# A second token mixer reorganised into a phase of paired block products and a phase of values, gates and small products

## The chip, the cores and the metric

The kernel runs on one core of one Trainium2 chip. The metric is the time on the device in microseconds (us), the median of several runs. The engines are named as in the profile: PE is the matrix engine (PEld its weight loads), DVE the vector engine, ACT the scalar engine, POOL the general engine, SP the engine that issues the DMAs. PE writes to PSUM, eight banks of 128 x 512 float32 elements. All other on-chip data lies in SBUF, 128 partitions wide.

## What is computed

A decoder trunk of two layers on 1024 tokens of width 1024. Layer 0 has a gated DeltaNet and a short convolution, layer 1, which this change concerns, has HGRN2 and dilated attention. Each layer ends with a SwiGLU feed-forward part of 2816 hidden columns. Cut to what matters:

```python
def mixer_cd(h, w_in, lower_bound, norm_g, w_out):          # h: 1024 x 1024, already normed
    hq, hf, hi, hg, sq, sk, sv = split_cols(h @ w_in, CD_SPLITS)   # 4 x 512 and 3 x 1536 columns
    f_gate = lb + (1.0 - lb) * sigmoid(hf)
    k_in = (1.0 - lb) * sigmoid(-hf)
    o_c = hgrn2_recurrence(silu(hq), k_in, hi, log(f_gate))  # 4 heads of 128, a chunked recurrence
    o_c = rms_norm(o_c, norm_g) * sigmoid(hg)
    sq, sk = rope(sq), rope(sk)                              # 3 patterns x 4 heads of 128
    for p, (window, dilation) in enumerate(((128, 1), (512, 4), (2048, 16))):
        outs[p], lses[p] = dilated_window_attention(sq[p], sk[p], sv[p], window, dilation)
    o_d = sum over p of outs[p] * softmax(lses)[p]
    return concatenate([o_c, o_d]) @ w_out
```

## The kernel before

**Products in three terms.** Activations and weights are float32. Each is split into a high part (a cast on ACT, line 101) and a low part (a subtraction on DVE, line 102), and a product is three matmuls: high by high, high by low, low by high (lines 125 to 127). A column block is 128 output columns with all 1024 rows of depth, that is 8 depth steps. The 1024 tokens are two halves of 512. So a column block costs 2 x 8 x 3 = 48 matmuls of 512 columns.

**The feed-forward part** (class `Up`, from line 251) already does less. It takes two column blocks at once, a gate and an up block, as a 2 x 2 block product (column block by depth half) with the 2 x 2 blocks of the activations (depth half by token half), with seven block products in place of eight and sums and differences around them: weights get the sums s1 to s4 (POOL, lines 296 to 302), activations the sums t1 to t4 (`turn`, line 586 on DVE). The names a11, a12, a22 are weight blocks, b11, b21, b22 activation blocks. `pair` is one round: p1, p2, row 2, row 1, p6, p5, p7, where PE's, DVE's, ACT's, POOL's and, after the first rounds, SP's instructions stay in the order in which they are written (`manual_schedule`).

**The second mixer** (`mixer_cd`, from line 1375) does not. In it the order is set by a planner, which lays the instructions of each engine in a row beforehand, by their priority (the order in which the program names them) and by planned durations. On the chip each engine then goes through its row and waits where an input is late. The program names the work as wide products with small work between them:

- `hgrn_fq`: forget and query tiles of an HGRN2 head, two column blocks.
- `hgrn_v`: HGRN2 values of two heads, 128 tokens at a time, matmuls of 256 columns.
- `swa_v`: attention values of a pattern for four heads, matmuls of 512 columns.
- `swa_qk`: query and key blocks of one head and pattern, then the rotary step (lines 1656 to 1663: two copies on ACT that swap the halves, two products and a sum on DVE), kept in SBUF.
- `hgrn_gates`: the gates of HGRN2.

Between wide products `tick(cost)` lets two generators go one step each per unit of cost: `chain`, the HGRN2 units (a head and a token half) in ten steps (`hgrn`, lines 1452 to 1600: forget preparation with a reciprocal at 1458 and a scan at 1461, seven levels of decayed copies at 1473 to 1481, small products at 1489 to 1595), and `local`, the attention (`Attend`: scores at 1706 with the masked minimum at 1713, transposes at 1752, outputs at 1763, and for pattern 0 the merge of the three patterns at 1801 to 1824). A unit of cost is one token half of a column block, 24 matmuls. The output projection (`out_proj`) needs all tiles of a token half from DRAM, attention tiles first.

PSUM banks have three tags: g (2 banks, HGRN2 steps), u (3 banks, wide products) and m (3 banks, attention).

## Time and profile before

| what | value |
|---|---|
| three runs | 2606.16, 2606.19 and 2607.6 us; median 2606.19 us |
| profiled execution, first to last instruction (its span) | 2604.6 us, so 1.6 us less than the median run |
| PE busy | 2585.2 us, 99%, 14355 matmuls |
| DVE, ACT, POOL busy | 1651.8, 1006.9 and 462.6 us |
| data moved by DMA | 402.98 MB |
| second mixer, 1155 to 1862 us | 707.00 us, with DVE busy 446.96 us |

The page of the profile has busy totals, then the span in 40 slices with a digit for the busy tenths of each engine, then the chain of work that ended last. The view by windows gives busy time and counts of each engine in stretches of time; the view by line gives groups of instructions with their total and mean duration and the idle time before them. A matmul's recorded duration is longer than its distance from the next one, since they are pipelined.

### The profile page before, as it was taken

What the parts mean: (1) busy time and instruction counts of PE and PEld (TensorE: products, weight loads), DVE (VectorE), ACT (ScalarE), POOL (GpSimd) and SP (SyncE); (2) the same over time, 40 slices, a digit from 0 to 9 for tenths busy, and PEclk for the clock granted to TensorE, in tenths of its full rate; (3) what the DMA queues carried; (4) which work ended last, traced back from release to release, by engine and by line L of the source; (5) the groups of instructions that cost most, each with busy time, mean ns of one, the idle gap of its engine ahead of it and who ended that gap; (6) DMA issues with size and microseconds to landing.
All of it is one profiled execution on the core that took longest, in us unless ns stands there. A gap on an engine that the chain in (4) does not pass through costs nothing.

```text
span 2604.6 us, 37378 instructions
## 1 busy us (share of the span) xinstructions
PE 2585.2 (99%) x14355; PEld 2159.7 (83%) x14355; DVE 1651.8 (63%) x2816; ACT 1006.9 (39%) x1679; POOL 462.6 (18%) x436
## 2 busy tenths in 40 slices
PE   8999999999999999999999999999999999999998
PEld 6888888888888888888888888888888888888887
DVE  7887776585656665564665557578567565566554
ACT  5432123343333345333444335444444333334442
POOL 1110121334333300010000000000024433331001
PEclk9999999999999999999999999999999999999999
DMA  4434446424556688541212222224652555568853
GB/s 143 134 103 151 123 143 202 166 88 163 183 186 202 217 292 293 189 134 62 81 62 74 86 70 62 86 70 126 219 195 68 174 174 200 204 205 284 281 173 120
DMA packets 239827, 402.98 MB, mean 155 GB/s; under 512 B 30208, under 2 KB 114720, under 8 KB 239520
## 3 DMA queue, kind: packets, MB, share of 16 engines
q1 hardware_dynamic: 239648, 400.59, 46.3%
q8 instruction: 113, 1.85, 0.3%
q14 instruction: 66, 0.54, 0.1%
HBM read 280.36 MB, written 120.14 MB: 154 GB/s over the span
## 4 chain that ended last, share of the span: by engine, by line
PE 95%; DVE 3%; issue 1%; ACT 0%; DMA 0%; POOL 0%; SPq 0%; POOLq 0%; DVEq 0%; ACTq 0%
PE psu L125 20%; PE psu L127 20%; PE psu L126 20%; PE psg L125 5%; PE psg L127 5%; PE psg L126 5%; PE psm L127 4%; PE psm L125 4%; PE psm L126 4%; PE psm L1763 1%; PE psm L1706 1%; PE psg L1489 1%; PE psm L198 1%; DVE h L586 1%; PE psm L1752 0%
## 5 line engine op out<-in xcount | busy, mean ns | idle before, releaser
L125 PE MATMUL psu<-hnh,w 128*128 128x512 f32 x1328 | 531.0, 400 | 7.1 <-ACT w L101 7.1
L127 PE MATMUL psu<-hnh,w 128*128 128x512 f32 x1328 | 520.1, 392 | 0.0
L126 PE MATMUL psu<-hnl,w 128*128 128x512 f32 x1328 | 519.2, 391 | 0.5 <-DVE hnl L1928 0.5
L102 DVE TENSOR_TENSOR w<-raw,w 128x1024 fp32r<-128x1024 f32 (+1 forms) x314 | 372.3, 1187 | 154.6 <-ACT w L101 152.5
L101 ACT CAST w<-raw 128x1024 fp32r<-128x1024 f32 (+1 forms) x314 | 306.1, 976 | 301.5 <-PE psu L127 153.4
L125 PEld LDWEIGHTS psu<-hnh,w 128*128 128x128 f32 x1328 | 250.4, 189 | 57.1 <-ACT w L101 7.1
L127 PEld LDWEIGHTS psu<-hnh,w 128*128 128x128 f32 x1328 | 249.9, 188 | 53.9 <-DVE w L102 0.8
L126 PEld LDWEIGHTS psu<-hnl,w 128*128 128x128 f32 x1328 | 250.5, 189 | 50.2 <-DVE hnl L1928 1.1
L186 POOL TENSOR_TENSOR acc<-acc,sq 128x512 f32<-128x512 f32 x48 | 70.6, 1471 | 497.9 <-ACT sq L182 497.9
L102 DVE TENSOR_TENSOR hidq<-hr,hidq 128x1024 fp32r<-128x1024 f32 x72 | 82.4, 1146 | 71.2 <-ACT hidq L101 70.8
L296 POOL TENSOR_TENSOR ws<-raw 128x512 f32<-128x512 f32 x40 | 54.4, 1360 | 356.3 <-DMA raw<-in_dram 254.2
L125 PE MATMUL psu<-w,hnh 128*128 128x512 f32 (+1 forms) x320 | 113.3, 354 | 0.0
L102 DVE TENSOR_TENSOR w<-ws,w 128x1024 fp32r<-128x1024 f32 x38 | 49.7, 1308 | 98.9 <-ACT w L101 98.9
L127 PE MATMUL psu<-w,hnl 128*128 128x512 f32 (+1 forms) x320 | 111.4, 348 | 0.0
L126 PE MATMUL psu<-w,hnh 128*128 128x512 f32 (+1 forms) x320 | 111.3, 348 | 0.0
L101 ACT CAST hidq<-hr 128x1024 fp32r<-128x1024 f32 x72 | 70.2, 980 | 97.3 <-DMA hr<-ts 56.8
L125 PE MATMUL psm<-hidq,w 128*128 128x512 f32 (+1 forms) x275 | 106.1, 386 | 0.0
L127 PE MATMUL psm<-hidq,w 128*128 128x512 f32 (+1 forms) x275 | 106.0, 385 | 0.0
L126 PE MATMUL psm<-hidq,w 128*128 128x512 f32 (+1 forms) x275 | 106.0, 385 | 0.0
L1527 POOL COPY attn<-ac 32x128 f32<-32x128 f32 x32 | 12.8, 401 | 433.3 <-DVE ac L1493 380.5
L125 PE MATMUL psu<-hidq,w 128*128 128x512 f32 (+1 forms) x220 | 84.7, 385 | 0.0
L127 PE MATMUL psu<-hidq,w 128*128 128x512 f32 (+1 forms) x220 | 84.6, 384 | 0.0
(451 smaller groups left out, 5744.9 us busy)
## 6 DMA issues: line engine op xcount, KB each, us to landing
raw<-in_dram SPq DMA_DIRECT2D x228, 512.0 KB, 3.7
sd<-in_dram SPq DMA_DIRECT2D x44, 512.0 KB, 3.8
hid<-hid SPq DMA_DIRECT2D x88, 256.0 KB, 2.9
sd<-sd SPq DMA_DIRECT2D x44, 512.0 KB, 3.3
hr<-ts SPq DMA_DIRECT2D x40, 512.0 KB, 4.6
raw<-sd SPq DMA_DIRECT2D x40, 512.0 KB, 3.9
hd<-h SPq DMA_DIRECT2D x48, 256.0 KB, 4.0
h<-hd SPq DMA_DIRECT2D x48, 256.0 KB, 5.8
```

The lines of the kernel that those rows point to most:

```text
L101: S.copy(hi, src)
L102: eng.tensor_tensor(lo, src, hi.bitcast(F32), op=SUB)
L125: T.matmul(o, lh, rh, start=first and i == 0, stop=False, **kw)
L126: T.matmul(o, lh, rl, start=False, stop=False, **kw)
L127: T.matmul(o, ll, rh, start=False, stop=last and i == n - 1, **kw)
L186: (eng or G).tensor_tensor(a, a, q, op=ADD)
L198: T.matmul(st[:, j:j + 1], x[:, j * P:(j + 1) * P], onesn, start=i + j == 0, stop=i == 1, skip_group_check=True)
L296: G.tensor_tensor(s[:, HT:], b[:, :HT], b[:, HT:], op=ADD)
L586: eng.tensor_tensor(dst, x, y, op=SUB)
L1489: T.matmul(od[r * 32:(r + 1) * 32, c * 32:(c + 1) * 32], a[:, z], x[:, z], start=True, stop=True, tile_position=(0, r * 32))
L1706: T.matmul(o[:, z], self.q[:, j * P:(j + 1) * P], self.k[:, (j - m + 1) * P:(j + 1) * P], start=True, stop=True)
L1763: T.matmul(po[:, jj * P:(jj + 1) * P], pt[:, z.start + i * P:z.start + (i + 1) * P], self.vp[:, j - m + 1 + i, :], start=i == 0, stop=i == ...
```

## The change

Before the mixer's values, a new class `Pairs` goes through 16 pairs of column blocks with the seven block products of `Up`: 12 pairs are the query and key blocks of a head and pattern, 4 are the forget and query blocks of an HGRN2 head. The four results of a pair (two blocks by two token halves) are finished by generators that are stepped between the products: `roped`, `forget` and `query`. One of the two rotary products moves from DVE to POOL. The finished tiles are stored to DRAM. `turn` now ends in a method `ends`, which each class has for itself, and hands one block of activations (b12) to `upper`, which stores it; at the end of the pairs it is loaded again into the tiles of t1, so that the normed activations are whole for the values.

`mixer_cd` then has values, gates and all small products. `ask` loads the tiles of an HGRN2 unit, `Attend` loads its own queries, keys and values, one head and pattern ahead. The scan, which ran over 512 columns with a mask that reset it, runs in four pieces of 128 in `forget`. `tick` now counts for the two generators at different rates, and its costs are in half units of before (12 matmuls). The gates are made head by head, both token halves.

```diff
+    class Pairs(Up):
+        early = True
+        HEADS = (("k", 0, 0), ("k", 0, 1), ("k", 0, 2), ("k", 0, 3), ("k", 1, 0), ("f", 0), ("k", 1, 1), ("k", 1, 2),
+                 ("f", 1), ("k", 1, 3), ("k", 2, 0), ("f", 2), ("k", 2, 1), ("k", 2, 2), ("f", 3), ("k", 2, 3))
...
+        def upper(self, b12):
+            dma(self.b12, b12)
...
+        def done(self, f, i, half, c, psum=False):
+            kind = self.HEADS[f]
+            if kind[0] == "k":
+                return self.roped(self.qk[kind[1:]][i, :, half], kind[1], half, c, psum)
+            if i == 0:
+                return self.forget(self.bkq[kind[1], half], kind[1], c)
+            return self.query(self.bkq[kind[1], half], c, psum)
+
+        def roped(self, dst, p, half, c, psum):
+            t = slice(half * HT, (half + 1) * HT)
+            r = self.turned()
+            S.copy(r[0:64], c[64:128])
+            S.copy(r[64:128], c[0:64])
+            G.tensor_tensor(r, r, self.rope[:, 1, t], op=MULT)
+            V.tensor_tensor(c, c, self.rope[:, 0, t], op=MULT)
+            yield
+            if p == 0:
+                d = r if psum else c
+                V.tensor_tensor(d, c, r, op=ADD)
+            else:
+                n = (None, 4, 16)[p]
+                d = self.scratch("d")
+                V.tensor_tensor(d.rearrange("p (r i) -> p i r", r=n), c.rearrange("p (i r) -> p i r", r=n),
+                                r.rearrange("p (i r) -> p i r", r=n), op=ADD)
+            dma(dst, d)
+            yield
+
+        def forget(self, dst, h, c):
+            r = self.turned()
+            V.tensor_scalar(c, c, -44.0, None, op0=MAX)
+            S.activation(r, c, AF.Exp, scale=-1.0)
+            S.activation(c, r, AF.Identity, bias=onec[:, 0:1])
+            yield
+            V.reciprocal(c, c)
+            d = self.scratch("d")
+            G.tensor_tensor(d, r, c, op=MULT)
+            yield
+            S.activation(r, c, AF.Ln, scale=self.omlb[:, h:h + 1], bias=self.lb[:, h:h + 1])
+            S.activation(d, d, AF.Copy, scale=self.omlb[:, h:h + 1])
+            dma(dst[1], d)
+            yield
+            for j in range(4):
+                t = slice(j * P, (j + 1) * P)
+                V.tensor_tensor_scan(c[:, t], onec[:, 0:1].to_broadcast([P, P]), r[:, t], 0.0, op0=MULT, op1=ADD)
+            dma(dst[0], c)
+            yield
...
+        def pair(self, f, count, b11, b21, b22, t1, t2, t3, t4):
+            n = f + 1
+            more = n < count
+            self.p1(f, b11)
+            self.add22(f - 1)
...
+                an = self.next
+                bn = self.raw("u", n, n % 3 == 2)
+            c = self.done(f - 1, 1, 1, self.c22.pop(f - 1))
+            next(c)
+            self.p2(f, b21, psm())
+            g = self.snap(f)
+            next(self.tail, None)
+            next(c)
+            next(self.tail, None)
...
+            if more:
+                s = self.sums(an, bn)
+            self.add11(f, g)
+            g = self.done(f, 0, 0, self.g1.pop(f))
+            next(g)
+            if more:
+                self.part_a(n, an)
+            x = self.row2(f - 1, t4)
+            next(x)
+            next(g)
+            z = self.row1(f - 1, b22)
+            next(x)
+            if more:
+                self.sums_late(an, bn, s)
+                if f > 3:
+                    self.part_b(n, s)
+            self.p6(f, t2)
...
+            next(z)
+            next(g, None)
+            self.p5(f, t1, psg())
+            if more:
+                if n + 1 < count:
+                    self.next = self.raw("g", n + 1, (n + 1) % 3 == 1)
+                slow = self.HEADS[f - 1][0] == "f"
+                if slow:
+                    next(z)
+                self.part_c(n, bn)
+                self.part_d(n, an)
+                next(g, None)
...
+                self.tail = z
+                self.p7(f, t3)
+                return
...
-    def mixer_cd(hn, hp, second, close):
+    def mixer_cd(hn, hp, pairs):
...
-                    tick(0.5)
+                    tick(1)
...
+            def ask(u):
+                if u < 8:
+                    h, half = divmod(u, 2)
+                    raws[u] = [hl(n, bufs=2) for n in ("b", "kk", "q")]
+                    for i, t in enumerate(raws[u]):
+                        dma(t, pairs.bkq[h, half][i])
...
-            def hgrn_gates():
+            def hgrn_gates(tick):
                 ws = [wload(("cd", 12 + 2 * i), ("cd", 13 + 2 * i)) for i in range(2)]
-                for half in range(NH):
-                    for h in range(4):
-                        oc = hl("e4", bufs=3)
+                for h in range(4):
+                    for half in range(NH):
+                        o = proj(wk(ws[h // 2], h % 2), hn[half], range(KH), last=False)
+                        tick(1)
+                        proj(wk(ws[h // 2], h % 2), hn[half], range(KH, KT), o, first=False)
+                        xg = hl("xg", bufs=2)
+                        S.activation(xg, o, AF.Tanh, scale=0.5)
+                        tick(1)
+                        while done_c[0] <= 2 * h + half:
+                            next(hg_chain, None)
+                        oc = hl("oc")
                         dma(oc, scr_g[half, h])
...
-                        tick(0.75 if len(tts) > 1 else 1)
+                        tick(1.5 if len(tts) > 1 else 2)
...
-                def __init__(self, h, p, q, k, vp):
+                def __init__(self, h, p):
+                    self.h, self.p = h, p
+                    for i, n in enumerate("qk"):
+                        t = tl(n, (2, HT), 2)
+                        if p == 2 and i == 0:
+                            t4 = t.rearrange("p b t -> p (b t)").rearrange("p (s b i) -> p b s i", s=16, b=2)
+                            for b in range(2):
+                                dma(t4[:, b], pairs.qk[p, h][i, :, b].rearrange("p (s i) -> p s i", s=16))
+                        else:
+                            dma(t, pairs.qk[p, h][i])
+                        setattr(self, n, t)
+                    self.vp = values(h, p)
...
-            acc = [0.0]
+            due, rate = [0.0, 0.0], [0.0, 4 / 3]
 
             def tick(cost):
+                for i in range(2):
+                    due[i] += cost * rate[i]
+                while max(due) >= 1:
+                    for i, work in enumerate((loc, hg_chain)):
+                        if due[i] >= 1:
+                            due[i] -= 1
+                            next(work, None)
...
+            hgrn_v(0, pairs.first, lambda cost: None, range(0, 4))
+            have_v[0] = 1
+            hgrn_v(0, pairs.first, tick, range(4, 8))
             for p in (1, 2, 0):
                 swa_v(p, tick)
-                feed_hgrn()
-                for h in range(4):
-                    q, k = swa_qk(h, p, tick)
-                    ready.append([Attend(h, p, q, k, values(h, p)), 0])
-                    feed_hgrn()
...
+                ready += [(h, p) for h in range(4)]
+                rate[0] = 1.4 if p == 0 else 0.8
+                if p == 2:
+                    hgrn_v(1, wload(("cd", 10), ("cd", 11)), tick)
+                    have_v[0] = 2
+            hgrn_gates(tick)
             while ready or busy[0]:
                 next(loc)
```

More of the change, by code (lines that the diff above doesn't have):

```diff
@@ L252, in hybrid_trunk_kernel @@
     class Up:
+        early = False
         def __init__(self, layer, left):
@@ L1859, in local @@
                     line = [line[1], nxt]
-                    busy[0] = any(line) or bool(late)
+                    busy[0] = any(line) or bool(late or now or ahead or ready)
                     yield
```

340 lines of the change are left out of this document (216 added, 124 removed).

## The prediction

> **What bounds the kernel now.** The page first: engine totals, slices, and the chain that ended last.
>
> ```profile
> span 2604.6 us, 37378 instructions
> PE 2585.2 (99%) x14355; PEld 2159.7 (83%) x14355; DVE 1651.8 (63%) x2816; ACT 1006.9 (39%) x1679; POOL 462.6 (18%) x436
> PE   8999999999999999999999999999999999999998
> DVE  7887776585656665564665557578567565566554
> PEclk9999999999999999999999999999999999999999
> PE 95%; DVE 3%; issue 1%; ACT 0%; DMA 0%; POOL 0%; SPq 0%; POOLq 0%; DVEq 0%; ACTq 0%
> ```
>
> PE is busy in every slice at the full granted clock, and the chain is PE for 95%. A busy PE need not be a PE at its rate, so next come stages, from the view by windows: the turn of the first feed-forward part, the pairs that follow it, the whole second mixer, and a piece near its end.
>
> ```profile
> core 0: us, PE busy (x) PEld busy (x) DVE busy (x) ACT busy (x) POOL busy (x), PEclk, DMA share, GB/s
> 530.00:565.00 35.00, 34.27 (x150) 27.74 (x149) 34.75 (x33) 18.19 (x23) 9.51 (x3) 1.00 0.16 51
> 565.00:980.00 415.00, 415.00 (x1833) 343.88 (x1832) 250.03 (x322) 150.87 (x204) 132.24 (x98) 1.00 0.61 207
> 1155.00:1862.00 707.00, 707.00 (x5378) 598.76 (x5379) 446.96 (x1043) 307.27 (x639) 26.23 (x51) 1.00 0.27 84
> 1740.00:1780.00 40.00, 40.00 (x416) 34.13 (x415) 36.88 (x106) 23.03 (x53) 2.15 (x4) 1.00 0.31 93
> ```
>
> Between 565 and 980 all products have 512 columns: 415.00/1833 = 0.2264 us each. The gate multiplications on POOL come once a pair there; the first and the fourth of a run of four:
>
> ```profile
> 702.06 1.29 POOL L387 TENSOR_TENSOR hid<-hid,c 128x512 f32<-128x512 f32 x1 [0.18 <-ACT hid L386]
> ...
> 759.18 1.29 POOL L387 TENSOR_TENSOR hid<-hid,c 128x512 f32<-128x512 f32 x1 [0.36 <-ACT hid L386]
> ```
>
> Three pairs in 57.12 us are 19.04 each, and 84 x 0.2264 = 19.02: the scheme that the change extends already runs without a stall in this kernel. In the mixer I count 1,536 products of 512 columns for queries, keys, forget tiles and HGRN2 queries, 576 for attention values and 192 for gates: 2,304 x 0.2264 = 521.6 of 707 us; the narrow value products and small ones are the other 185. PE never lacks work there, so removed products come off the end, as long as what remains still has cover.
>
> **The sum.** A pair of column blocks costs 2 blocks x 2 halves x 8 depths x 3 terms = 96 products now, and 7 x 4 x 3 = 84 as block products. 16 pairs save 192 x 0.2264 = **-43.5 us**. Against it:
>
> *Turn.* Building the four sums of activations is the same code as before the feed-forward pairs. Its window above has 150 products, 34.0 us of work in 35.00, with DVE busy 34.75. The second half's norm, which it takes in, was in the old mixer too. I add **+1** (0 to +2).
>
> *Phase one: 16 pairs on in-order queues.* DVE costs are read from a dense piece of its timeline, since recorded spans overlap:
>
> ```profile
> 1229.33 0.43 DVE L1477 TENSOR_TENSOR m<-m,kk 128x256 f32<-128x256 f32 x1
> 1229.67 0.42 DVE L1481 TENSOR_TENSOR m<-m,q 128x256 f32<-128x256 f32 x1
> 1230.01 0.69 DVE L1539 TENSOR_TENSOR kk<-kk,b 128x512 f32<-128x512 f32 x1
> 1230.61 0.69 DVE L1534 TENSOR_TENSOR q<-q,t 128x512 f32<-128x512 f32 x1
> ```
>
> Starts are 0.34 us apart for 256 columns and 0.60 for 512, about 0.09 below the spans. So I take 0.09 off the means of the groups by line (mixer window):
>
> ```profile
> L102 DVE TENSOR_TENSOR w<-raw,w 128x1024 fp32r<-128x1024 f32 x55 | 67.3, 1223 | 46.3 <-ACT w L101 46.2
> L101 ACT CAST w<-raw 128x1024 fp32r<-128x1024 f32 x54 | 56.6, 1047 | 26.4 <-PE psu L127 22.0 <-DMA raw<-in_dram 3.9
> L1659 DVE TENSOR_TENSOR sw<-sw,rope 128x512 f32<-128x512 f32 x48 | 33.1, 690 | 31.1 <-ACT sw L1657 29.0 <-DMA vp<-scr_v 1.8
> L1656 ACT COPY sw<-psu 64x512 f32<-64x512 f32 x48 | 28.0, 583 | 120.7 <-PE psu L127 87.0 <-issue 33.2 <-ACT attn L1524 0.4
> L1458 DVE RECIPROCAL b<-b 128x512 f32<-128x512 f32 x8 | 26.8, 3352 | 0.2
> L1473 DVE TENSOR_TENSOR m<-b 128x256 f32<-128x256 f32 x56 | 23.2, 420 | 24.4 <-PE psg L1489 24.1
> L1663 DVE TENSOR_TENSOR k<-psu,sw 128x512 f32<-128x512 f32 x24 | 22.9, 954 | 0.2
> L1461 DVE TENSOR_TENSOR_SCAN b<-rmask,t 128x512 f32<-128x512 f32 x8 | 9.8, 1222 | 4.8 <-ACT t L1460 4.7
> ```
>
> DVE per query/key pair: 3.5 splits of 1.13 (4.0), three additions of 0.60 (1.8), four rotated tiles of 0.60 + 0.87 (5.9): 11.7 of 19.0 us, 62%, where the feed-forward pairs have 250.03/415 = 60% and no stall. POOL takes one rotary product a tile; with four weight sums that is 8 x 1.29 = 10.3 of 19.0, and the weight sums queued behind them have half a pair to spare. ACT: 3.5 casts of 1.05, and three copies and eight half-height copies of 512 columns at 0.58: 10.1.
> A forget pair has 4.0 + 1.8 + 2 x (0.60 + 3.35 + about 1.5 for the scan in four pieces) + 2 x 0.60 = 17.9 on DVE. Forget pairs are three apart: (17.9 + 2 x 11.7)/57 = 72%. What queues behind the 3.35 us reciprocal is the next pair's weight splits, which PE reads at least four products (10.9 us) later, and the additions that free a PSUM bank. Cover gone, eight reciprocals would cost 27 us; I add **+2** (0 to +13, four exposed).
> SP gets some 72 more stores of 256 KB in front of weight loads; the stage before shows 61% DMA with PE full and the old mixer 27%, so 0.
>
> *Phase two: less cover.* PE keeps 707 - 1,536 x 0.2264 = 359 us of work. From DVE's 447 us go the rotary products (48 x (0.60 + 0.60 + 0.87) = 99), the forget preparation (8 x 6.9 = 55) and 32 weight splits (36): about 257 us stay. 72% on average; the end is denser, so I price it separately.
> *One HGRN2 unit* (head and half) on DVE: 26 half-width steps of 0.34 (8.8), seven of 0.60 (4.2), eleven small ones of about 0.2 (2.2): 15.2 us. The pacing now gives 4/3 of its ten steps per 12 wide products (2.72 us), where before it gave one per 24. Units 4 to 7 wait until the second pair's values exist, so all four meet the last stretch, together with attention pattern 0:
>
> ```profile
> L1713 DVE CUSTOM_DVE_ANT_0 sc<-psm,cf 128x256 f32<-128x256 f32 x44 | 18.2, 419 | 8.8 <-PE psm L1706 8.8
> L1817 DVE TENSOR_TENSOR ol<-ol,cm 128x512 f32<-128x512 f32 x16 | 11.0, 689 | 0.3
> L1814 DVE TENSOR_TENSOR cm<-cm,w 128x512 f32<-128x512 f32 x16 | 10.4, 689 | 0.0
> L1810 DVE TENSOR_TENSOR dn<-dn,tmp 128x4 f32<-128x4 f32 x16 | 2.6, 166 | 0.5
> ```
>
> Pattern 0 on DVE: 32 score reductions of 0.33 (10.6), eight copies and 40 merge products of 0.60 (28.8), 112 small ones of about 0.14 (15.7): 55 us. On PE, from the chain in order of time:
>
> ```profile
> 1747.47 0.66 PE psm L1706 x4
> 1748.13 0.44 PE psm L1752 x4
> 1748.56 0.89 PE psm L1763 x8
> 1749.46 0.96 PE psg L1489 x66
> 1756.10 0.86 PE psm L1706 x4
> ```
>
> A head's pattern 0 is about eight sets of keys (0.86 x 4 = 3.4 less the narrow ones: 1.6 for 8 blocks), 15 transposes, 15 outputs and 8 final transposes of 0.11: 5.8 us, 23 for four. A unit's small products are about 6.5.
> The gates stretch then holds on PE: 192 x 0.2264 = 43.5, 23 of pattern 0, and the 1.9 units that the pacing leaves (12): **79 us**. On DVE: 1.9 x 15.2 = 29, 55, gates 5, splits for the output projection 7: 96, of which some 12 (last unit, second half's merges) may follow: **84 us**. Below this density is proof: 36.88 of 40 us (92%) in the window 1740:1780 with PE full. At 92%, 84 becomes 91: 12 late, less 21 products (4.8 us) of the first projection block that run before its last input: **+8** (0 at full density, +20 at 80%). Before this stretch, four units and pattern 1 have 28% slack and a pause at the second values, so +0; the first attention loads come without a lead (up to +4).
>
> Sum: -43.5 + 1 + 2 + 8 = -32.5 on the profiled execution's span, 2604.6 to 2572.1. The median of the three runs, 2606.19, is 1.6 above the span: **2574**.
>
> *Table loads* on ACT bear on the forget pairs, which alternate Exp, Ln and Tanh (one line's instructions, first and last start):
>
> ```profile
> L1460 ACT ACT_TABLE_LOAD  x8: 1283/1283/1283, 1168.3 to 1701.2; - x8
> L1460 ACT ACTIVATE t<-b,lb,omlb x8: 813/816/821, 1169.6 to 1702.5; 128x512 f32<-128x512 f32 x8
> ```
>
> The load takes 1.28 us and its activation starts 1.3 us after it. ACT per forget pair: casts 3.7, three copies 1.7, two times four activations of 0.58 to 0.82 (5.2), two more for the queries (1.2), four loads (5.1): 17 of 19.0, no loss. The Trainium skill ("ScalarE: Activation LUTs", What ACT_TABLE_LOAD costs) adds a drain of about 1.38 us to each switch. By it, as an estimate, ACT would need 22.5 us (17 + 4 x 1.38) and each forget pair lose 3.5: 14 in all. These rows show no gap after the load; one ahead of it they can't exclude.
>
> **Rivals.**
> *Everything stays covered.* For it: no stage of the old kernel lets PE wait, not even at 92% DVE. Against: 84 against 79 us. Time: 2606.2 - 43.5 + 1 = 2564.
> *ACT bound in forget pairs* through costs at each table change beyond the 1.28: 3.5 us in each of four pairs, 2574 + 14 = 2588. For: 17 of 19 us are taken. Against: the rows just shown, and two light pairs between.
> *The gain is eaten*: DVE at 75% in the last stretch and four exposed reciprocals: 84/0.75 - 79 - 5 = 28, + 13 + 1: 2606.2 - 43.5 + 42 = 2605.
> *Slower: DVE can't be packed in phase two.* From unit 4 on, PE has about 143 us up to the output projection (wide 87, four units 26, patterns 2 and 0 7 + 23; pattern 2 scaled by its columns), DVE 132 (units 61, patterns 12 + 55, gates and splits 16, less the 12 that may follow). The chain of a unit alternates DVE, ACT and PE, and if it holds DVE to the 63% that it has over the old mixer (447/707), 132 take 210: 67 lost, 2606.2 - 43.5 + 1 + 67 = 2631. It decides below 132/(143 + 43.5) = 71%. Against: 92% and the turn's 99%; for: those are short, and PE's order is fixed beforehand with planned durations, so a late small product holds wide ones behind it.
> That the products aren't saved is excluded by the 19.04 us per pair.
>
> **Chances.** Forecast 0.52, all covered 0.20, table changes 0.06, eaten 0.07, slower 0.15. The first three are faster: 0.78. This kernel's runs differ by 0.06%; about 0.2%, 5 us, can be told from no change. "Eaten" is 0.07 within it, and slower 0.15. Low end 2562: full cover with no turn loss is 2562.7. High end 2606 takes in the eaten case; only the slower one lies outside. The forecast's own range is 2564 to 2586.
>
> **What would show it.** Right: a first phase of about 305 us + 1 with pairs 19.0 apart; 192 products fewer; a second phase of 359 us plus a gap of 0 to 20 only near the output projection, with DVE above 90% before it. Wrong step by step: pairs wider than 19.1 (reciprocal, or ACT at Ln); PE idle at small products earlier in phase two, released by DVE or ACT (the slower rival); waits on query or key loads; granted clock below 1.00 after a gap. A time under 2562 would mean that the old mixer lost time between products that I count as work.

## The result and the profile after

The changed kernel takes 2652.84 us (median of four runs, 2650.91 to 2653.08) against 2606.18 for the kernel before (four runs, 2606.13 to 2607.6): 1.0177 times as long, with an interval of 1.0162 to 1.0191. It is 46.7 us slower where 32 less were forecast. From the page: span and busy totals, PE and DVE in 40 slices, and the chain that ended last.

```profile
span 2651.3 us, 37844 instructions
PE 2571.7 (97%) x14163; PEld 2131.2 (80%) x14163; DVE 1750.8 (66%) x2873; ACT 1076.2 (41%) x1779; POOL 656.1 (25%) x552
PE   8999999999999999998888899999999999999998
DVE  7887775685655665578777776358867655556554
...
PE 37%; DVE 4%; issue 1%; ACT 1%; POOL 0%; DMA 0%; POOLq 0%; DVEq 0%; ACTq 0%
```

14,163 matmuls are 192 fewer, as forecast. But five slices of PE are at 8; these are the pairs. The chain's line can't be set beside the 95% of before: it gives shares of the span, and the chain in order of time starts at 1477 us, in the pairs. In its first 55 us, up to 1532, PE has 2.8 us and DVE 23.1; behind that it is mostly PE. The view by windows gives the new mixer in four pieces: the turn, the sixteen pairs, the second phase up to its gates, and the gates up to the output projection's norm. After the time come the busy times of PE, PEld, DVE, ACT and POOL with their counts, the clock, and DMA.

```profile
core 0: us, PE busy (x) PEld busy (x) DVE busy (x) ACT busy (x) POOL busy (x), PEclk, DMA share, GB/s
1155.00:1215.00 60.00, 55.89 (x243) 45.72 (x242) 55.19 (x55) 29.25 (x37) 21.18 (x11) 0.94 0.28 91
1215.00:1532.00 317.00, 273.19 (x1122) 215.61 (x1121) 235.01 (x234) 168.93 (x236) 165.78 (x102) 0.96 0.30 100
1532.00:1803.00 271.00, 265.23 (x2832) 225.72 (x2831) 156.78 (x479) 125.71 (x318) 26.22 (x42) 1.00 0.55 157
1803.00:1968.00 165.00, 158.44 (x1258) 133.32 (x1256) 125.13 (x370) 78.87 (x184) 15.86 (x18) 0.99 0.72 221
```

PE idles 43.8 us in the pairs and 12.3 in the second phase, and the clock in the pairs is 0.96. No other engine is full there: DVE 235.01/317 = 74%, ACT 53%, POOL 52%. The 74% looks like the 72% of the prediction, but that was for pairs 19 us apart, and this stretch has grown. Its 1,122 products need 254.0 us at 0.2264 each; of those DVE's 235.01 us would be 93%, ACT's 67% and POOL's 65%. So DVE is recorded with 17.6 us of work for each 84 products, where the sum had 11.7 for a query/key pair and 17.9 for a forget pair, 13.25 on average. It still fits, and yet PE waits.

To see the whole loss, half-rate matmuls included, I give each matmul the mean distance from its start to the next that its shape had in the mixer of before, and call what a stretch takes beyond the sum its *loss*. For before's own mixer the sum is 753.8 us and the stretch 753.3; single pieces are good to some 5 us. For the changed kernel:

| stretch | time | loss | forecast |
|---|---|---|---|
| turn, 1155 to 1215 | 60.0 | 7.6 | 1 |
| pairs, 1215 to 1532 | 317.0 | 59.1 | 2 |
| second phase before the gates | 271.2 | 11.8 | 0 |
| gates to the output projection's norm | 164.4 | 10.7 | 8 |

Less the 43.5 us of products that is 45.7 us, against 46.7 between the two spans (2651.3 and 2604.6).

The waits of PE over the whole run: who waits, on what; total, times and longest in us. Before has no such wait in its mixer.

```profile
engine line waited for: us in total, times, longest us
PE psu L126 <- ACT u L365: 24.4, 11, 4.9
PE psg L126 <- DVE c L826: 12.6, 10, 2.9
PE psu L126 <- ACT c L825: 8.5, 7, 1.8
```

L365 copies the PSUM bank of a pair's sixth product (p6), L825 copies the same bank after p7, and L826 adds the bank of p5 to that copy. These are the small steps that must have read a bank before PE goes on in it; over 16 pairs they were late 11, 7 and 10 times. Why, one pair shows in order of time (all engines; lines left out are marked):

```profile
1386.28 3.35 DVE L800 RECIPROCAL u<-u 128x512 f32<-128x512 f32 x1 [1.51 <-ACT u L798]
1387.61 0.58 ACT L825 COPY c<-psu 128x512 f32<-128x512 f32 x1
1389.55 2.85 DVE L103 TENSOR_TENSOR w<-raw,w 128x1024 fp32r<-128x1024 f32 x2
...
1392.32 0.67 DVE L826 TENSOR_TENSOR c<-c,psg 128x512 f32<-128x512 f32 x1
...
1393.03 0.62 ACT L778 COPY r<-c 64x512 f32<-64x512 f32 x1 [4.84 <-DVE c L826]
...
1394.30 0.59 ACT L338 COPY gt<-psu 128x512 f32<-128x512 f32 x1
...
1394.36 1.80 POOL L780 TENSOR_TENSOR r<-r,rope 128x512 f32<-128x512 f32 x1 [2.51 <-ACT r L779]
1394.91 1.28 ACT L804 ACT_TABLE_LOAD   x1
1396.12 1.30 POOL L302 TENSOR_TENSOR ws<-raw 128x512 f32<-128x512 f32 x1
1396.19 2.17 DVE L789 TENSOR_TENSOR d<-c,r 128x512 f32<-128x512 f32 x1 [1.19 <-POOL r L780]
1396.20 0.82 ACT L804 ACTIVATE r<-u,lb,omlb 128x512 f32<-128x512 f32 x1
...
1398.20 2.41 DVE L810 TENSOR_TENSOR_SCAN u<-onec,r 128x128 f32<-128x128 f32 x4
...
1400.54 0.66 DVE L342 TENSOR_TENSOR gt<-gt,psm 128x512 f32<-128x512 f32 x1
...
1401.28 0.62 ACT L778 COPY r<-gt 64x512 f32<-64x512 f32 x1 [3.64 <-DVE gt L342]
...
1404.82 1.05 ACT L102 CAST w<-ws 128x1024 fp32r<-128x1024 f32 x1
1405.77 0.58 ACT L365 COPY u<-psu 128x512 f32<-128x512 f32 x1
```

ACT copies tile c at 1387.61, but its sum on DVE (L826) stands behind the reciprocal and two weight splits and comes at 1392.32. ACT's next instruction in the written order needs that sum, so ACT stands 4.84 us. It then makes the swapped halves, POOL its product (L780), and DVE, whose next instruction needs that product, stands 1.19. So DVE reaches the next sum (L342) only at 1400.54, and ACT, which needs it next, stands 3.64. The copy of the sixth product (L365), for which PE waits, is queued behind all that. Each engine has a quarter or half of its time free, but spends it in turn waiting for another. The same view on PE shows what follows the copy:

```profile
1401.12 0.39 PE L128 MATMUL psg<-t1h,w 128*128 128x512 f32 x1
1406.40 0.79 PE L126 MATMUL psu<-t3h,w 128*128 128x512 f32 x1 [4.90 <-ACT u L365]
1406.99 0.63 PE L127 MATMUL psu<-t3l,w 128*128 128x512 f32 x1
1407.42 0.63 PE L128 MATMUL psu<-t3h,w 128*128 128x512 f32 x1
...
1410.40 0.42 PE L126 MATMUL psu<-t3h,w 128*128 128x512 f32 x1
1410.66 0.40 PE L127 MATMUL psu<-t3l,w 128*128 128x512 f32 x1
```

After the wait the starts are 0.43 us apart, and only from 1410.40 on 0.23 to 0.26: the granted clock has halved (the view by windows has 0.50 from 1406.40 to 1410.40). 60 such matmuls stand in the turn and the pairs, about 12 of the 66.7 us.

The pair shown is one of the slow ones. From the start of one pair's first product to the next pair's, the twelve rounds from 1216 to 1502 us take 19.5 to 30.1 us, 57 above twelve times 19.04. The three longest (30.1, 27.9 and 28.2) are those in which the second reciprocal of a forget pair stands (1312.1, 1386.3 and 1457.4); they hold 29 of the 57 us, the other nine some 3 each.

### The profile page after: what moved, and what is told of

Same layout as the page of the kernel before. It is cut to its first block, busy times and chain, and to the rows that moved or that the text cites. A ratio compares the mean times of both kernels' runs of the same rounds, so it can differ in the third digit from the quotient of the medians.

```text
span 2651.3 us, 37844 instructions
## 1 busy us (share of the span) xinstructions
PE 2571.7 (97%) x14163; PEld 2131.2 (80%) x14163; DVE 1750.8 (66%) x2873; ACT 1076.2 (41%) x1779; POOL 656.1 (25%) x552
## 5 line engine op out<-in xcount | busy, mean ns | idle before, releaser
L126 PE MATMUL psu<-hnh,w 128*128 128x512 f32 x848 | 338.4, 399 | 7.6 <-ACT w L102 7.6
L127 PE MATMUL psu<-hnl,w 128*128 128x512 f32 x848 | 332.0, 392 | 0.1
L128 PE MATMUL psu<-hnh,w 128*128 128x512 f32 x848 | 332.0, 391 | 0.0
L126 PEld LDWEIGHTS psu<-hnh,w 128*128 128x128 f32 x848 | 160.2, 189 | 40.1 <-ACT w L102 7.6
L128 PEld LDWEIGHTS psu<-hnh,w 128*128 128x128 f32 x848 | 159.8, 188 | 34.6 <-DVE w L103 0.8
L127 PEld LDWEIGHTS psu<-hnl,w 128*128 128x128 f32 x848 | 160.3, 189 | 32.7 <-DVE hnl L2162 0.7
L302 POOL TENSOR_TENSOR ws<-raw 128x512 f32<-128x512 f32 x54 | 75.7, 1403 | 399.0 <-DMA raw<-in_dram 255.4
L103 DVE TENSOR_TENSOR w<-ws,w 128x1024 fp32r<-128x1024 f32 x51 | 73.2, 1436 | 97.7 <-ACT w L102 97.7
L126 PE MATMUL psu<-t3h,w 128*128 128x512 f32 x240 | 98.7, 411 | 24.6 <-ACT u L365 24.4
L780 POOL TENSOR_TENSOR r<-r,rope 128x512 f32<-128x512 f32 x48 | 80.6, 1682 | 97.9 <-ACT r L779 90.9
L126 PE MATMUL psu<-t4h,w 128*128 128x512 f32 x240 | 95.0, 396 | 9.0 <-ACT c L825 8.5
L126 PE MATMUL psg<-b22h,w 128*128 128x512 f32 x216 | 85.8, 397 | 12.6 <-DVE c L826 12.6
L127 PE MATMUL psu<-t3l,w 128*128 128x512 f32 x240 | 96.7, 403 | 0.0
L128 PE MATMUL psu<-t3h,w 128*128 128x512 f32 x240 | 96.7, 403 | 0.0
```

Of the source, the lines that this page charges most:

```text
L103: eng.tensor_tensor(lo, src, hi.bitcast(F32), op=SUB)
L126: T.matmul(o, lh, rh, start=first and i == 0, stop=False, **kw)
L127: T.matmul(o, lh, rl, start=False, stop=False, **kw)
L128: T.matmul(o, ll, rh, start=False, stop=last and i == n - 1, **kw)
L302: G.tensor_tensor(s[:, HT:], b[:, :HT], b[:, HT:], op=ADD)
L780: G.tensor_tensor(r, r, self.rope[:, 1, t], op=MULT)
```

## The experiments

Theory A: the finishing steps of the tiles form one chain over ACT, POOL and DVE, and queues in a fixed order let a late step of one tile delay the PSUM copies of the next. Rivals for the pairs: B, the copy of the sixth product just stands behind a cast; C, the stores hold up the weight loads on SP; two that the prediction had, the reciprocals and the table loads of the forget tiles; and the amount of work on DVE. (The texts on record say TensorE, VectorE, ScalarE, GpSimd and SyncE for PE, DVE, ACT, POOL and SP.) "Pairs" below is turn and pairs together, 1154.7 us to the first value product: 377.5 us in the changed kernel; "second phase" runs from there to the output projection's norm: 435.6. The mark 1154.7 is kept for all kernels; where the stages ahead ended later (by 1.7 to 2.4 us in e2, e4 and e8 to e10) that is counted in "pairs". In the kernels with a planned order (e5, e6, e9 to e12, e14 to e16) the last 24 products of the pairs stand behind the first value product, which makes "pairs" 5.4 us shorter and the second phase as much longer.

| kernel | us | ratio to before, interval | pairs | second phase |
|---|---|---|---|---|
| changed | 2652.84 | 1.0177, 1.0162 to 1.0191 | 377.5 | 435.6 |
| e1_bare | 2589.36 | one run | 315.5 | 434.4 |
| e2_rope_dve | 2638.7 | 1.0120, 1.0103 to 1.0137 | 368.6 | 433.9 |
| e3_copy_first | 2651.51 | 1.0174, 1.0159 to 1.0189 | 378.1 | 434.2 |
| e4_late_stores | 2650.02 | 1.0165, 1.0150 to 1.0180 | 377.4 | 432.6 |
| e5_planned | 2642.8 | one run | 364.8 | 438.5 |
| e6_planned_dve | 2623.2 | one run | 344.2 | 439.1 |
| e7_values_early | 2665.35 | one run | 377.9 | 447.8 |
| e8_merge_pool | 2670.01 | one run | 380.0 | 450.1 |
| e9_all_three | 2621.81 | 1.0061, 1.0043 to 1.0079 | 340.3 | 439.7 |
| e10_slow_chain | 2624.76 | one run | 342.7 | 442.7 |
| e11_copies_ahead | 2623.4 | one run | 344.7 | 438.8 |
| e12_late_row | 2606.88 | 0.9998, 0.9989 to 1.0007 | 326.8 | 437.5 |
| e13_late_row_alone | 2662.11 | 1.0212, 1.0196 to 1.0228 | 388.7 | 433.7 |
| e14_no_merge | 2604.02 | one run | 328.4 | 436.3 |
| e15_no_forget_chain | 2538.33 | one run | 325.3 | 373.1 |
| e16_no_windows | 2514.86 | one run | 325.2 | 349.8 |

**e1_bare**: the rotary step of queries and keys without its swapped halves, sine product and sum.

```diff
-            S.copy(r[0:64], c[64:128])
-            S.copy(r[64:128], c[0:64])
-            G.tensor_tensor(r, r, self.rope[:, 1, t], op=MULT)
-            V.tensor_tensor(c, c, self.rope[:, 0, t], op=MULT)
+            V.tensor_tensor(r, c, self.rope[:, 0, t], op=MULT)
             yield
...
-            dma(dst, d)
+            dma(dst, r)
```

> Leaves out part of the computation: a query or key tile is only multiplied by the cosine and stored (no swapped halves, no sine product on POOL, no sum); the forget pairs, the block products and the whole second phase stay. The stretch of the 16 pairs with its turn took 375 us (1155 to 1530) where the products alone are 305. If the finishing of the tiles holds PE (theory A: a serial chain through DVE, ACT and POOL in queues that keep their order), the stretch falls to 310 to 325 and the time to 2590 to 2605. If the block products or their weight loads hold it themselves (rival), it stays above 350 and the time above 2630.

The pairs take 315.5 us, 62 less, and the loss in the sixteen pairs is gone: the rounds take 19.0 us each. The pairs by windows:

```profile
1215.00:1470.00 255.00, 252.78 (x1115) 208.64 (x1114) 176.85 (x189) 117.30 (x150) 94.00 (x57) 1.00 0.37 122
```

PE is full, the clock 1.00. Block products, weight sums, weight loads, stores and all of the forget preparation with its eight reciprocals and table loads are still there, so none of these costs anything by itself. But the edit also takes 58 us of busy time from DVE and 72 from POOL, so it does not yet tell the chain from the amount of work. What remains is in the turn (about 5 us) and the second phase, which did not move.

**e2_rope_dve**: the sine product from POOL to DVE.

```diff
-            G.tensor_tensor(r, r, self.rope[:, 1, t], op=MULT)
+            V.tensor_tensor(r, r, self.rope[:, 1, t], op=MULT)
```

> Undoes one part: the sine product goes back from POOL to DVE, 48 instructions. Theory A with POOL as the costly link (1.7 us a product, and DVE instructions beside it recorded up to twice as long): the stretch of the pairs shrinks by 25 to 45 us, the time to 2608 to 2628, although DVE gets 29 us more work. Rival, order on ACT alone: within 5 us of 2653. If DVE's amount of work is the bound, slower: 2665 to 2680.

14 us faster, where theory A had 25 to 45, although DVE now has the more to do: the link over POOL is one cause, but not the greater part.

**e3_copy_first** and **e4_late_stores**, rivals B and C. The first puts the split of the weight sums behind the copy of the sixth product. The second holds each store of a finished tile until the next weight load is issued.

```diff
                 self.sums_late(an, bn, s)
-                if f > 3:
-                    self.part_b(n, s)
             self.p6(f, t2)
-            if f == 3:
+            if more:
                 self.part_b(n, s)
```

```diff
-            dma(dst, d)
+            self.put(dst, d)
...
                 bn = self.raw("u", n, n % 3 == 2)
+            self.flush()
```

> One part moved: the split of the next pair's summed weights is put behind the copy that empties the PSUM bank between the sixth and the third product, as it stands in the first pair already. Theory B (that copy waits on ACT behind a cast which waits for POOL's weight sums; 24.4 us of PE's waits name the copy): 15 to 25 us faster, 2628 to 2638. Theory A alone: 0 to 8 us faster, since the chain is late anyway.

> One part moved: on SP the stores of finished tiles are held back and issued behind the next weight load, so that no load queues behind a store that waits for DVE. Theory C (weight loads late, POOL's weight sums wait 28 us for them between 1215 and 1530): 10 to 25 us faster, 2628 to 2643. Theories A and B alone: within 5 us of 2653, or slower where a buffer comes free later.

Both fall. In e3 PE's wait for L365 fell from 24.4 to 16.6 us, while that for L825 rose from 8.5 to 18.6: the loss only changed its place. In e4 the pairs kept their 377 us.

**e5_planned** and **e6_planned_dve**: in the pairs only PE keeps the written order, and the planner orders DVE, ACT, POOL and SP; e6 has the sine product on DVE as well.

```diff
-            with tc.manual_schedule(engines={E.PE, E.DVE, E.Activation, E.Pool, E.SP}):
+            with tc.manual_schedule(engines={E.PE}):
                 self.p7(2, t3)
```

> Same instructions; in the pairs only PE's order is kept as written, and DVE, ACT, POOL and SP are put in order by the planner, as in the old mixer. Theory A (the written order makes a serial chain between engines that are each no more than 74% busy): most of the 62 us that the bare finishing gave back come back here too, the pairs fall from 377 to 320 to 350 us, the time to 2595 to 2625. Rival (amount of work with DVE and POOL slowing each other): within 10 us of 2653, since the amounts are the same.

> As the one before, and the sine product on DVE. If the order is the chain and POOL's link is long: another 5 to 15 us under it. If DVE's amount then binds (233 of 315 us busy before, some 29 more): 0 to 15 us above it.

10 us for the order alone, 29.6 for both. e5 is a miss for theory A, which had 2595 to 2625, and lies at the edge of its rival (within 10 us of 2653): another order of the same work does little as long as the sine product is on POOL. e6 is 19.6 us under e5, more than the 5 to 15 expected. That both edits together give more than the 24 us that they give singly would fit a chain over queues, but 5.6 us between single runs don't show it; the four runs of e2 spread over 4.8. PE's remaining waits in the pairs of e6 were for L365 alone.

**e7_values_early** and **e8_merge_pool** asked whether DVE is overfull beside the gates in the second phase: one takes the second pair's HGRN2 values, and with them chain units 4 to 7, one attention pattern earlier, the other moves the 24 merge products to POOL.

```diff
-                if p == 2:
+                if p == 1:
                     hgrn_v(1, wload(("cd", 10), ("cd", 11)), tick)
```

```diff
-                    V.tensor_tensor(t[p][:, :, 0:P], t[p][:, :, 0:P],
+                    G.tensor_tensor(t[p][:, :, 0:P], t[p][:, :, 0:P],
```

> Phase two alone: the second pair of HGRN2 values is made after the first pattern's values instead of after the second's, so that units 4 to 7 no longer wait and leave the last stretch. The time from the first values to the norm of the output projection is 435.6 us, where the same work took about 419 in the old order. Theory of the tail (DVE overfull in the gates stretch): 8 to 18 us less. Rival (phase two lags by the chain of each HGRN2 unit wherever it stands): within 4 us.

> Phase two alone: the 24 merge products of 512 columns (0.60 us each on DVE, about 14 us) go to POOL, which is 6% busy in that stretch. Theory of the tail: 4 to 12 us less. If POOL slows DVE beside it as it did in the pairs, or the merge's own latency ends the stretch: 0 to 10 us more.

Both are slower, by 12 and 17 us, outside everything that was expected. In e7 the loss before the gates grew from 11.8 to 21.0, in e8 that beside the gates from 10.7 to 24.8. So taking work from DVE beside the gates did not help. That steps which come closer together (e7) or take longer (e8) cost time would fit both, but these two runs don't show it.

**e9_all_three**, **e10_slow_chain**, **e11_copies_ahead**: e9 is e6 with the edits of e3 and e4. To it e10 adds a slower forget chain in the second phase, and e11 gives the copies and sums of PSUM banks priority in the planner.

```diff
-            due, rate = [0.0, 0.0], [0.0, 4 / 3]
+            due, rate = [0.0, 0.0], [0.0, 1.0]
```

```diff
-            S.copy(s, self.x[f])
+            with tc.high_priority(offset=200):
+                S.copy(s, self.x[f])
```

> In the pairs: the sine product on VectorE, only TensorE's order by hand (the two edits of the kernel that took 2623.2), and with them the copy of the sixth product ahead of the next pair's weight split and each store held until the next weight load is issued. What is left in that kernel is read as a late weight path: GpSimd's weight sums waited 89.6 us for the raw weight loads and SyncE 88.6 us for the tiles that it stores. If the stores in front of the loads are the cause, this kernel gains what is left of the pairs' loss, 15 to 25 us: 2598 to 2608. If the chain on ScalarE and VectorE itself is what is late, holding the stores changes nothing, as it changed nothing alone: 2618 to 2628.

> The kernel e9_all_three with one more edit, in the second phase: the forget chain is stepped once for each step of the products instead of 4/3 times. The pairs should take the same time. If the second phase loses its 15 to 20 us because the chain stands too densely beside the products, slower steps give back 5 to 12 us of it. If the loss belongs to the amount of work on VectorE over the whole phase, the steps left over pile up beside the gates and the time stays the same or grows by up to 10 us.

> The kernel e9_all_three with the copies of the sixth product and of the third tile's PSUM bank, and the sum behind the latter, given priority over other ready work of ScalarE and VectorE. If the wait of TensorE for these copies is only a matter of where they stand among ready work, the pairs lose 10 to 20 us less. If what the copies wait for is the weight path or a chain that is late as a whole, less than 4 us.

e9 is 1.4 us from e6, so the stores are not it either, and e11 gains nothing. What PE still waits for in e9, nine times in the pairs, and ACT's timeline at one of them:

```profile
PE psu L126 <- ACT u L365: 21.8, 9, 4.4
```

```profile
1322.64 0.62 ACT L779 COPY r<-u 64x512 f32<-64x512 f32 x1 [3.00 <-DVE u L847]
1323.27 0.62 ACT L780 COPY r<-u 64x512 f32<-64x512 f32 x1
1323.91 0.58 ACT L365 COPY u<-psu 128x512 f32<-128x512 f32 x1
```

ACT waits 3.00 us for a sum on DVE and swaps its halves, and the copy for PE stands behind them. That sum belongs to row 1 of the pair before, whose product PE computes directly ahead of the sixth one. The planner, too, had put the two swapped halves ahead of the copy. In e10 the loss before the gates fell from 10.1 us (e9) to 3.6, beside the gates it rose from 11.0 to 20.6: the second phase loses where the chain's steps are dense. As a whole e10 is 3 us slower than e9, not 5 to 12 faster: the steps left over pile up beside the gates, which was the rival's forecast.

**e12_late_row** and **e13_late_row_alone** move that product of row 1 behind the sixth one, in e9 and in the changed kernel as it is.

```diff
-            z = self.row1(f - 1, b22)
             next(x)
...
             self.p6(f, t2)
+            z = self.row1(f - 1, b22)
```

> The kernel e9_all_three with the fourth row's product of the pair before (the 12 products into the second tile's bank) moved from in front of the sixth product to behind it, so that the copy of the sixth product has two products instead of one to hide behind, and the turned halves of the moved product come after that copy. If the place of that product causes the waits, the 21.8 us of waits in the pairs go to under 6 and the rest of the clock's slow stretches with them: 2593 to 2602, under the kernel before. If the finishing chain as a whole is late, the wait moves on to the next product: over 2612.

> The changed kernel as it is (every engine in the written order, the sine product on GpSimd) with only that product moved behind the sixth one. If the product's place is the whole cause of the pairs' 59 us, 2600 to 2610. If the chain over three engines in written order is, the waits move to other products and a few us are won: 2635 to 2650.

In e12 the wait for L365 in the pairs falls from 21.8 to 9.7 us (under 6 was expected) and the pairs to 326.8. The kernel takes as long as the one before, 0.9998 times (0.9989 to 1.0007), not less as I expected. Alone, the same move costs 9 us, where both theories had it faster: in e13 PE waits for other copies (`gt` of L338 19.2 us, `c` of L825 18.8). So it is not the place of one product either: the move pays only with the other edits. PE's waits and the pairs of e12:

```profile
PE psu L126 <- ACT u L365: 9.7, 7, 4.9
```

```profile
1215.00:1481.00 266.00, 254.26 (x1098) 206.80 (x1097) 236.53 (x274) 165.31 (x230) 86.11 (x57) 0.99 0.36 121
```

DVE has 236.53 us of work here, a little more than the 235.01 of the changed kernel, in 266 us instead of 317: 89% busy, and PE waits less than at 74%. Its 1,098 products need 248.6 us, so this is the same amount of work on DVE for each product, or a little more (95%), with some 45 us less in the pairs (the 24 products counted in). So the amount of work on DVE isn't what cost that time. Nor is the reciprocal alone: no round in which one stands takes over 20.9 us here.

**e14_no_merge**, **e15_no_forget_chain**, **e16_no_windows** take out of e12 most of the merge's work on DVE, the forget chain, and the windows' small products.

```diff
-                    V.tensor_tensor(t[p][:, :, 0:P], t[p][:, :, 0:P],
-                                    w3[:, p, :, None].to_broadcast([P, 4, P]), op=MULT)
-                    if p:
-                        V.tensor_tensor(t[0][:, :, 0:P], t[0][:, :, 0:P], t[p][:, :, 0:P], op=ADD)
+                    if p == 2:
+                        V.tensor_tensor(t[0][:, :, 0:P], t[1][:, :, 0:P], t[p][:, :, 0:P], op=ADD)
```

```diff
                 b, kk, q = raws.pop(2 * h + half)
+                dma(scr_g[half, h], q)
+                yield
+                return
```

> The kernel e12_late_row without most of the merging of the three windows' results in the second phase: the 24 products on VectorE and half of their sums are left out. If VectorE's load in the second phase is what takes the 17 to 21 us, the phase loses 8 to 14 us less, most of it beside the gates; if the latency of the steps is, under 4 us.

> The kernel e12_late_row with the forget chain of the second phase left out (its eight units store their query tile as a result; no levels, states or normalization). The phase must become shorter by the chain's own products; what counts is the time that it takes over its products at the kernel before's mean steps, 19 us in e12. If the chain's steps stand too close for their latency, 0 to 6 us of that is left. If the windows' steps or the weights are at fault, 12 to 19.

> The kernel e12_late_row with the windows of the second phase left out (scores, weights, their outputs and the merge; the value products stay). Over its products' own time the phase lost 19 us in e12. If the windows' steps are at fault, 0 to 6 us of that is left; if the forget chain's are, 12 to 19.

Without the merge work the second phase takes 1.2 us less, so this load of DVE is not the cause. Its loss was 18.9 us in e12, 4.1 without the forget chain and 14.5 without the windows. These sums can't say which part has more: the 4.1 are 9.1 beside the gates and -5.0 before them, so the mean steps are off by that much where the mix of narrow products changes. PE's idle time in the windows is firmer. First e12's second phase, up to the gates and beside them:

```profile
1481.00:1756.00 275.00, 270.79 (x2858) 230.34 (x2858) 160.73 (x485) 129.96 (x324) 27.49 (x41) 1.00 0.53 152
1756.00:1919.00 163.00, 156.61 (x1254) 131.56 (x1253) 125.97 (x371) 79.32 (x184) 15.43 (x18) 1.00 0.72 226
```

Then e15 (without the chain) and e16 (without the windows):

```profile
1480.00:1704.00 224.00, 224.00 (x1372) 193.67 (x1372) 59.85 (x209) 84.25 (x231) 3.18 (x4) 1.00 0.64 189
1704.00:1853.00 149.00, 141.98 (x743) 118.94 (x742) 98.28 (x290) 67.36 (x158) 8.76 (x6) 0.99 0.74 238
```

```profile
1480.00:1712.00 232.00, 228.85 (x2477) 193.11 (x2475) 134.02 (x310) 88.89 (x161) 30.59 (x41) 1.00 0.37 122
1712.00:1830.00 118.00, 115.63 (x946) 94.30 (x944) 72.27 (x131) 47.38 (x76) 17.88 (x18) 1.00 0.65 214
```

Before the gates PE idles 4.2 us in e12, never without the chain, and 3.2 us with the chain alone, although DVE is then at 58%: that piece is the chain's. Beside the gates it idles 6.4 us in e12, 7.0 without the chain and 2.4 without the windows, so that piece is mainly the windows' own; in e15 PE waits 6.5 us there for merged tiles.

## Why the prediction was wrong

*The products.* Right: 192 fewer, and in e1 turn and pairs take 315.5 us where 306 were forecast for a cover that holds.

*Turn, +1 (0 to +2).* 7.6 us, about 5 in e1. The prediction counted the second half's norm as neutral, since the old mixer had it too. There other products stood beside it; here PE waits for its row, and starts again at half rate:

```profile
1163.74 1.25 PE L213 MATMUL psm<-cf,r 128*128 128x128 f32 x8 [2.28 <-POOL r L204]
1164.65 0.76 PE L126 MATMUL psu<-hnh,w 128*128 128x512 f32 x1
1165.21 0.63 PE L127 MATMUL psu<-hnl,w 128*128 128x512 f32 x1
```

*Phase one, +2 (0 to +13).* This is the step that failed: 59 us. It asked of each engine whether its work fits into a pair's 19 us, and bounded the loss by reciprocals with their cover gone. The work does fit, but with less room than the sum had: against the products' own time DVE is at 93%, not at about 70, since the sum took each engine's durations alone and put the slowing of DVE and POOL by each other (below) at nothing. e12 does the work at 89% of its stretch with some 45 us less loss. What the prediction left out is that the work is a chain. A rotated tile goes from ACT to POOL and DVE and then DVE, and each stands in its queue at a written place. The words "the weight sums queued behind them have half a pair to spare" took a POOL instruction to start when POOL is free, but in the trace POOL waits for its operand (waits from 1215 to 1530 us; total, times, longest):

```profile
POOL r L780 <- ACT r L779: 68.9, 22, 8.0
ACT r L778 <- DVE c L826: 36.6, 8, 6.0
...
DVE d L789 <- POOL r L780: 20.5, 11, 4.6
```

The feed-forward pairs, which I used as proof, have the same products and, by the sum, nearly the same share of DVE (60 against 62%). But their gate multiplication on POOL is followed by a DVE instruction only a pair or two later (which waited for it 1.2 us in all from 565 to 980), and POOL is busy 32% there against the sum's 54. e1, e2, e6 and e12 bear this out step by step: 62 us without the chain, 14 without its POOL link, 30 with the link and the order changed, 46 with e3's and e4's edits and one product moved as well.

*Reciprocals and table loads.* Both were bounds or rivals. e1 and e12 show that neither costs much by itself. In the changed kernel the reciprocal is part of what stands in front: an exposed one was bounded at 3.35 us, but the three rounds named above are 9 to 11 us too long. The table load in the timeline above starts 0.02 us after the copy ahead of it ends (1394.30 + 0.59) and the activation 1.29 after that. So the drain of about 1.38 us that the Trainium skill ("ScalarE: Activation LUTs", What ACT_TABLE_LOAD costs) adds does not show here.

*SP, 0.* Right within what e4 can tell: 3 us.

*Phase two, +8 beside the gates and +0 before.* 10.7 and 11.8. The size beside the gates is near, but that is luck: its reason was DVE overfull, and there DVE is busy 125.13 of 165 us (76%), and with most of the merge gone (e14) the phase gains 1.2 us. Before the gates the slack of DVE was taken for cover; without the chain PE doesn't idle there (e15), and with steps at 1 instead of 4/3 for each 12 products it idles 1.3 us (e10) instead of 4.3 (e9). So the steps come faster than they follow one another.

*The slower rival* had the sign (2631) and nearly the mechanism, a chain between engines under an order of PE fixed beforehand, but put it in phase two, where it makes 22 us, instead of in the pairs, where it makes 59. It got 0.15 because short windows with a full PE beside a DVE at 92% spoke against it. They showed that a queue can be packed when its inputs are there, not that they will be.

What stays open: how much of the 59 us is waiting in order and how much is DVE and POOL slowing each other (below). The order alone gave 10 us (e5), the sine product off POOL, which shortens the chain and spares DVE at once, 14 (e2), and the rest came only with several edits together. Open, too, are the last 17 us between e12's pairs and e1's (326.8 + 5.4 against 315.5), of which one round of 26.7 us holds 8.

## What to carry to other kernels

Busy shares tell whether work fits, not whether it arrives, and a share of a stretch that has grown hides how nearly full an engine is: put its busy time beside the time that the products alone need. Before moving a step between engines, follow one tile through every queue that it passes, and ask at each instruction what is written behind it and who waits for that. A step that frees a PSUM bank should stand ahead of anything that waits for another engine, and a proof from another stage holds only if its chains have the same links. When a change loses time, a version without the suspected chain (here 62 us in one run) tells more than moving single instructions, which may only move the wait; a second one with the same load on the busiest engine, but other links and another order (e12), then tells the chain from the load.

## What the hardware showed

**DVE and POOL slow each other.** The same instruction on DVE, with one input from PSUM and with both from SBUF, in the pairs of the changed kernel (mean in ns after the total):

```profile
L781 DVE TENSOR_TENSOR u<-u,rope 128x512 f32<-128x512 f32 x9 | 14.4, 1605 | 1.0 <-ACT r L779 1.0
...
L781 DVE TENSOR_TENSOR psu<-psu,rope 128x512 f32<-128x512 f32 x8 | 5.5, 690 | 0.0
```

In the timeline above, the sum L789 starts at 1396.19 and takes 2.17 us instead of the mean of 1.09 that the same sum has with an input from PSUM; POOL's sum L302 ends at 1397.42, and from there 1.09 is 1398.51, near the sum's end at 1398.36. Two SBUF inputs alone are not slow: in before the same product took 690 ns with both from SBUF (L1659). The Trainium skill ("SBUF — State Buffer", Who interferes with whom) says that a DVE instruction with two SBUF inputs contends with a POOL instruction that reads SBUF, over ports that it calls an exclusive lock, and that a DVE instruction with at most one SBUF input, outside its two-port modes, does not: the trace agrees. So a weight split, which reads two, pays as well, as half-width splits in the feed-forward pairs of before and in the pairs of after show:

```profile
L102 DVE TENSOR_TENSOR w<-raw,w 128x512 fp32r<-128x512 f32 x21 | 14.4, 684 | 0.0
```

```profile
L103 DVE TENSOR_TENSOR w<-raw,w 128x512 fp32r<-128x512 f32 x11 | 13.0, 1178 | 0.0
```

The prediction's durations were those of instructions alone, 0.60 us on DVE and 1.29 on POOL.

**A wait of a few us costs its length and then some.** In e12 a wait of 2.5 us (L834 in the turn) is followed by six matmuls at half rate and one of 4.9 by eleven, 0.2 us lost on each. It isn't so each time: the same wait in the turn of e1, also 2.5 us, is followed by full rate. The Trainium skill ("TensorE: Matmul & The Clock Gate", Part 1) gives an idle window of about 3.4 us and as long a stretch of work to recover; the recovery is near the 4.0 us from 1406.40 to 1410.40 (about 3 and 5 us in e12), but waits shorter than the window sufficed here.
